# Later query maxima, key and value loads of layer 0 in pieces with two buffers, and a moved key copy in a two-layer attention backbone

## The chip, the cores and the metric

The kernel runs on one core of one Trainium2 chip. The metric is device time in microseconds (us) of one execution. The program is one launch of some 22,000 instructions on five engines: TensorE (PE: matrix products and transposes), VectorE (DVE), ScalarE (ACT), GpSimd (POOL) and SyncE (SP), which only issues DMA transfers. Each engine takes its instructions strictly in order; between engines they are tied by semaphores.

## The reference, cut to what matters

A context of 256 tokens and 1024 latent tokens (a 16 x 64 grid) of width 1024 pass through two layers. Each layer norms and modulates its input, projects it, runs two mixers side by side, gates them with SiLU and projects back.

```python
# layer 0 (even), for each of its two head groups A and B: 8 query heads, 2 key/value heads, head width 64
aq, ak, av, ag, bq, bk, bv, bg = split_cols(h @ w_in, EVEN_WIDTHS)
aq, ak = rms_norm(heads(aq), q_gain), rms_norm(heads(ak), k_gain)    # A alone; A and B get rotary
oa = gqa_attend(q_block, concat(c_ak, ak), concat(c_av, av))         # A: 128 queries against all 1280 keys
ob = gqa_attend(q_block, concat(c_bk, band of 384), ..., bias, sink) # B: context + window of +-128, a sink logit
y  = concat(oa * silu(ag), ob * silu(bg)) @ w_out
# layer 1 (odd): conformer convolution (C) and 2-D neighbourhood attention (D, 8 heads, 8 x 16 window + context)
y  = concat(conformer_conv(...), od * silu(dg)) @ w_out

def gqa_attend(q, k, v, bias, sink):
    s = einsum(q, k) * 64 ** -0.5 + bias
    return softmax(concat(s, sink)) @ v
```

Layer 0 also does the context rows; layer 1 updates the latent rows alone, and a last RMSNorm gives the output. All is float32.

## The kernel before, in words

Values keep float32 accuracy by being split into a high and a low part (`split`): a product is three matrix products of such parts. Everything that TensorE does is therefore in pieces of 128 x 128 by up to 512 columns.

**Layer 0** runs four *passes*, one for each pair of a mixer (B, then A) and a key/value head, in the sequence `ORDER = (2, 3, 0, 1)`. Ahead of a pass stands its projection, `fill0`: `proj_qkv` makes queries, keys and values for ten blocks of 128 tokens, and `proj_gate` the gate (the rest of it follows inside the pass). For each block `qk_tail` (L805 to L813) transposes queries and keys, splits them on ScalarE (`qs`), and SyncE writes them to DRAM: `Qd` at L812, `Kd` at L813. Values go to `Vd`, gates to `Gs`. The projections of the next pass are the *fill* that is woven into the attention of the pass that runs (`weave`): `NFILL = (39, 39, 36)` says how many steps of it.

A pass then has ten *groups*, one for each block of 128 queries (four heads wide, so 512 columns), in the sequence `QORD = (2, 3, 4, 0, 5, 6, 1, 7, 8, 9)`. A group is prepared by `attn_prep` (L365): it loads its queries (`load_q`: `QH`, twice the high part, and `QL`, the low part; three buffers each), makes its row maxima (`maxes`, products called `mx`, at L552 and below in layer 0 and at L1304 and below in layer 1, reduced on VectorE into `mp`), transposes the negated maxima (`trn`, L389) and writes them into `QL`. Then for each *key tile* of 128 keys `attn_gen` (L396) makes scores `st` from two products (L448 with the keys `KA`: high part in 64 partitions, low part in 64; L452 with `KB`: high part again, plus rows of ones that bring in the maxima), their exponential `pf` on ScalarE (L458 to L460), its two parts `ph` (ScalarE) and `pl` (VectorE or GpSimd), and, three tiles later (`flush`), three products with the values `V` into `ov` (L411 to L413). The last of a group's tiles ends with its normalisation and `finish`, which writes `Od`.

Groups are prepared two ahead: while group *g* runs through its key tiles, the preparation of *g*+2 advances with it, a few steps per tile (`g.step`); its first step issues the query load and the next four do nothing (`for _ in range(4): yield`).

The keys of a pass are loaded whole, when the pass's first group is prepared (`load_ka`, L520, two transfers of 64 x 1280 into one of two `KA` buffers) and when it starts (`load_kb`, L525, one more into the only `KB`); the values, whole, at its first `flush` (`load_v`, into the only `V` buffer).

**Layer 1** has sixteen groups (8 heads, two halves of 512 queries), with the projections of later heads and the output projection as fill. `load_head` (L1253) fetches the next head's keys at the start of a head's first group, and `load_k` (L359) does so with two transfers into `KA` and a copy of the high part into `KB` on ScalarE (L363).

What the program lists is not yet the order on the engines. The framework's scheduler builds each engine's order from the program's, by priorities and a timeline model of its own; the orders shown below are what it built.

Of the kernel before, what the change touches and what calls it, by code (L numbers as in the profile page):

```python
# [10 lines left out]
F32 = mybir.dt.float32  # L11
# [21 lines left out]
BMO = (0, 320, 320, 760)  # L33
LOOK0, LOOK1 = 3, 3
AHEAD = 3
BMB = 2
# [31 lines left out]
GB = 2  # L68
NFILL = (39, 39, 36)
GL = 12  # L70
# [18 lines left out]
def tile_kernel(ctx: ExitStack, tc: tile.TileContext, a, out):  # L89
# [268 lines left out]

    def load_k(k, kh, kl):  # L359
        KA, KB = Ks[k % len(Ks)]  # L360
        SY.dma_start(KA[0:64, :].bitcast(F32), kh)
        SY.dma_start(KA[64:128, :].bitcast(F32), kl)
        SC.copy(KB[0:64, :], KA[0:64, :].bitcast(F32))  # L363

    def attn_prep(pool, g):  # L365
# [28 lines left out]
    def attn_gen(pool, groups, vshare, look, nexts=None):  # L394
# [31 lines left out]

        for p in preps[:2]:
            for n_, _ in enumerate(p):
                if n_ % 2:
                    yield  # L430
        for gi, g in enumerate(groups):
            ids = [gi + 2] if gi + 2 < len(groups) else []
            if nexts is not None and gi in nexts:
                ids = nexts[gi]
            g.next = chain.from_iterable(preps[k] for k in ids)
            g.step = -(-18 * len(ids) // len(g.tiles))
        for g, t in items[:AHEAD]:
            g.ahead(t)
        for x, (g, t) in enumerate(items):
            if x + AHEAD < len(items):  # L440
                items[x + AHEAD][0].ahead(items[x + AHEAD][1])
            if t == 0:
                g.start()
            k, q0, n, extra = g.tiles[t]
            KA, KB = g.k()
# [30 lines left out]
            yield  # L476
# [40 lines left out]

    KAs, KBs = [None] * 4, [None] * 4

    def load_ka(u):  # L520
        KAs[u] = a0.tile([P, NTOK], F32R, tag="KA", name=nm("KAt"), bufs=2)
        SY.dma_start(KAs[u][0:64, :].bitcast(F32), Kd[u][:, 0, :])
        SY.dma_start(KAs[u][64:128, :].bitcast(F32), Kd[u][:, 1, :])

    def load_kb(u):  # L525
        KB = KBs[0]
        SY.dma_start(KB[0:64, :].bitcast(F32), Kd[u][:, 0, :])

    def group0(u, qb):
        isb = u >= 2  # L530

        first = qb == QORD[0]

        def load_q(QH, QL):
            if first:
                load_ka(u)
            src = Qd[u][qb].rearrange("(e d) s a t -> d s e (a t)", e=2)
            for dst, s in ((QH[0:64, :], 0), (QH[64:128, :], 0), (QL[0:64, :], 1)):
                SY.dma_start(dst.bitcast(F32).rearrange("d (e c) -> d e c", e=2), src[:, s])
# [6 lines left out]
        def maxes(QH, mp):  # L546
# [12 lines left out]
            for hd in range(4):  # L559
# [7 lines left out]
                else:  # L567
# [30 lines left out]
        def finish(ov, rb):  # L598
# [9 lines left out]
            else:  # L608
# [3 lines left out]

        hs = (u - 2) * 4
        g = Group(load_q=load_q, start=(lambda: load_kb(u)) if first else (lambda: None), bias=False, ahead=lambda t: None, gate=gate, v=lambda k: Vs[0][:, k, :], load_v=(lambda: SY.dma_start(Vs[0][:, :, 0:128].bitcast(F32), Vd[u])) if first else None, maxes=maxes, nmp=1 if qb < 2 else (2 if isb else 3),
                  sink=(sink[:, hs : hs + 4], sink8[:, hs : hs + 4]) if isb else None, skm=lambda: sk, k=lambda: (KAs[u], KBs[0]),
                  tiles=[(k, 0, 512, x) for k, x in kt], den=den, finish=finish)
# [6 lines left out]
    with ExitStack() as p0x:  # L623
# [181 lines left out]
        def qk_tail(u, j, pc):  # L805

            tr = bank("tr", nm("trk"))
            for i in range(3):
                PE.transpose(tr[:, i * P : (i + 1) * P], pc[:, i * P : (i + 1) * P], ident)
            qs = ap.tile([P, 2, 384], F32R, tag="qs", name=nm("qs"), bufs=2)  # L810
            split(tr[:, 0:384], qs[:, 0, :], qs[:, 1, :], "s", "v")
            SY.dma_start(Qd[u][j].rearrange("p a b t -> p a (b t)"), qs[:, :, 0:256].bitcast(F32))  # L812
            mark[0] = SY.dma_start(Kd[u][:, :, j * P : (j + 1) * P], qs[0:64, :, 256:384].bitcast(F32))  # L813

# [17 lines left out]
        def fill0(k, w=None):  # L832
            yield from proj_qkv(ORDER[k], w)
            yield from proj_gate(ORDER[k], gblocks(k)[0])

# [3 lines left out]
        while hold[0]:  # L839
            next(mods)  # L840
        v_tiles(a0, 10)
        KBs[0] = a0.tile([P, NTOK], F32R, tag="KB", name="KBt")
        GP.memset(KBs[0][64:68, :].bitcast(F32), 1.0)
        main = attn_gen(a0, [group0(u, qb) for u in ORDER for qb in QORD], VS0, LOOK0)
# [219 lines left out]
    with ExitStack():  # L1064
# [186 lines left out]
        od = [None, None]  # L1251

        def load_head(hd):  # L1253
            i, e = divmod(hd, 2)
            ds = slice(e * 64, (e + 1) * 64)
            load_k(hd, KD[i][ds, 0, :], KD[i][ds, 1, :])

        def group1(gi, hd, hf):
# [66 lines left out]
            def finish(ov, rb):  # L1325
# [6 lines left out]
                if i == 3:  # L1332
# [3 lines left out]

            g = Group(load_q=load_q, maxes=maxes, nmp=2, bias=True, ahead=ahead, sink=None, tiles=tiles, den=den, finish=finish,
                      start=start, gate=gate,
                      k=lambda: Ks[hd % len(Ks)], load_v=None, v=lambda k: Vs[gi % 2][:, k if k < 2 else k - 5 * hf, :])
# [4 lines left out]
        groups1 = [group1(gi, *x) for gi, x in enumerate(SEQ)]  # L1344
        load_head(0)
        x2, ocs, od3, fin = [], [], [], [0]

# [247 lines left out]
```

## Time and profile before

| | before |
|---|---|
| runs (us) | 1596.81, 1595.64, 1587.97; median 1595.64 |
| profiled execution (us) | 1590.95 |
| its span on the core (us) | 1589.2 |
| mean granted TensorE clock | 0.965 |
| bytes moved by DMA | 222 MB, mean 140 GB/s |

The profile is of one execution of its own, 1590.95 us of device time; the span is the part of it from the first to the last instruction. "Busy" is the time in which an engine executes, and what it waits for is told by the semaphore that ended the wait. In a row of the waits stand the engine, the operation and line that waited, what it waited for, then the total in us, the number of times and the longest. In a row of the timeline stand the start, the duration, the engine, the line, the operation, output <- inputs, shapes, and in brackets the idle time ahead of it with what ended that. The names are those of the program without their numbers: `KAt`, `KBt`, `Vt` are the tiles of keys and values, `Q`, `K`, `V`, `G` the DRAM buffers of layer 0, `QD`, `KD` those of layer 1.

### The profile page before, as it was taken

The numbers are of one execution on the slowest core, as the hardware profiler recorded it, in microseconds if no ns is written. First come the engines' busy times: TensorE is split into PE (matmuls) and PEld (weight loads), VectorE is DVE, ScalarE is ACT, GpSimd is POOL, SyncE is SP. The second block draws the span as 40 slices with busy tenths as digits, with TensorE's granted clock in tenths as the row PEclk, the third lists the DMA queues.
The fourth block names the chain that finished last, engine by engine and source line by source line (L and its number), as shares of the span: only waits on it lengthen the run. The fifth ranks groups of instructions, "written<-read, shape, count | busy, mean of one in ns | idle before, by whom it ended". The sixth has DMA issues, their size and how long they took to land.

```text
span 1589.2 us, 22236 instructions
## 1 busy us (share of the span) xinstructions
PE 1459.0 (92%) x6984; PEld 1180.6 (74%) x6984; DVE 1124.1 (71%) x2172; ACT 756.6 (48%) x1542; POOL 831.3 (52%) x760
## 2 busy tenths in 40 slices
PE   6789989998999988989999889999999999789895
PEld 1779867787778667767887768888887787577685
DVE  4898787588857668455478776999846467576676
ACT  2722353444434664654555564443433455545473
POOL 1561364455636667756654655754532334444575
PEclk9999999998999999989999989999999999799997
DMA  9548234532442123471111122213456878888732
GB/s 316 179 144 270 83 101 138 176 95 80 146 143 75 36 65 113 156 223 51 57 40 44 57 66 79 92 55 107 162 176 219 246 222 262 239 219 232 221 97 106
DMA packets 198462, 222.01 MB, mean 140 GB/s; under 512 B 18812, under 2 KB 154696, under 8 KB 198344
## 3 DMA queue, kind: packets, MB, share of 16 engines
q1 hardware_dynamic: 191680, 209.02, 42.9%
q10 hardware_dynamic: 6664, 11.57, 2.4%
q8 instruction: 55, 0.90, 0.2%
q14 instruction: 63, 0.52, 0.1%
HBM read 160.49 MB, written 60.03 MB: 139 GB/s over the span
## 4 chain that ended last, share of the span: by engine, by line
PE 61%; DVE 15%; DMA 13%; issue 4%; POOL 3%; SPq 2%; ACT 1%; DVEq 0%; POOLq 0%; ACTq 0%
PE p L320 6%; PE p L319 6%; PE p L321 6%; PE ov L411 4%; PE ov L413 4%; PE ov L412 3%; PE po L320 3%; PE po L319 3%; PE po L321 3%; PE st L448 3%; PE st L452 3%; DMA mw<-in_mod_w_dram 3%; DMA QH<-QD 2%; PE pq L321 2%; PE pq L319 2%
## 5 line engine op out<-in xcount | busy, mean ns | idle before, releaser
L300 POOL TENSOR_TENSOR pl<-pf,ph 128x512 fp32r<-128x512 f32 (+4 forms) x321 | 394.1, 1239 | 304.4 <-ACT ph L297 252.4
L300 POOL TENSOR_TENSOR wl<-wr,wh 128x256 fp32r<-128x256 f32 (+2 forms) x256 | 199.3, 794 | 218.2 <-ACT wh L297 209.4
L460 ACT ACTIVATE pf<-st 128x512 f32<-128x512 f32 x284 | 166.2, 596 | 171.3 <-PE st L452 126.5
L297 ACT CAST ph<-pf 128x512 fp32r<-128x512 f32 (+4 forms) x364 | 209.9, 588 | 38.4 <-PE ov L412 22.0
L297 ACT CAST wh<-wr 128x256 fp32r<-128x256 f32 (+2 forms) x264 | 103.4, 404 | 162.4 <-DMA wr<-in_od_d_dram 38.6
L319 PE MATMUL p<-hh,wh 128*128 128x512 f32 x448 | 177.2, 397 | 2.4 <-DVE spk L300 1.4
L320 PE MATMUL p<-hl,wh 128*128 128x512 f32 x448 | 178.4, 399 | 0.4 <-POOL hl L300 0.4
L321 PE MATMUL p<-hh,wl 128*128 128x512 f32 x448 | 173.3, 396 | 0.2 <-POOL wl L300 0.2
L411 PE MATMUL ov<-ph,Vt 128*128 128x512 f32 (+4 forms) x364 | 144.8, 398 | 15.4 <-DVE y L602 8.2
L413 PE MATMUL ov<-pl,Vt 128*128 128x512 f32 (+4 forms) x364 | 144.5, 397 | 7.5 <-POOL pl L300 5.5
L448 PE MATMUL st<-QH,KAt 128*128 128x512 f32 (+4 forms) x364 | 142.5, 393 | 5.4 <-ACT pf L460 3.4
L412 PE MATMUL ov<-ph,Vt 128*64 128x512 f32 (+4 forms) x364 | 142.0, 390 | 0.0
L452 PE MATMUL st<-QL,KBt 68*128 68x512 f32 (+4 forms) x364 | 137.5, 387 | 0.7 <-DVE QL L390 0.7
L1081 DVE SCALAR_TENSOR_TENSOR cps<-U,taps,cps 128x512 f32<-128x512 f32 x184 | 124.3, 747 | 0.0
L565 DVE TENSOR_REDUCE mp<-mx 128x1 f32<-128x512 f32 x128 | 85.9, 683 | 49.7 <-PE mx L564 49.1
L220 DVE SCALAR_TENSOR_TENSOR macc<-mw,csil,macc 128x512 f32<-128x512 f32 x107 | 93.1, 889 | 23.5 <-DMA mw<-in_mod_w_dram 21.4
L319 PEld LDWEIGHTS p<-hh,wh 128*128 128x128 f32 x448 | 84.1, 188 | 23.4 <-DVE spk L300 1.6
L321 PEld LDWEIGHTS p<-hh,wl 128*128 128x128 f32 x448 | 84.4, 189 | 20.5 <-POOL wl L300 0.6
L320 PEld LDWEIGHTS p<-hl,wh 128*128 128x128 f32 x448 | 84.2, 188 | 19.5 <-POOL hl L300 0.8
L411 PEld LDWEIGHTS ov<-ph,Vt 128*128 128x128 f32 x364 | 71.9, 197 | 32.9 <-issue 8.6
L413 PEld LDWEIGHTS ov<-pl,Vt 128*128 128x128 f32 x364 | 71.6, 197 | 31.5 <-POOL pl L300 8.5
L321 PE MATMUL pq<-wh,hl 128*128 128x384 f32 x256 | 88.7, 348 | 1.1 <-DVE hl L311 0.7
(276 smaller groups left out, 3521.5 us busy)
## 6 DMA issues: line engine op xcount, KB each, us to landing
mw<-in_mod_w_dram SPq DMA_DIRECT2D x34, 512.0 KB, 5.6
Q<-qs SPq DMA_DIRECT2D x40, 256.0 KB, 2.7
QH<-Q SPq DMA_DIRECT2D x80, 128.0 KB, 2.8
wr<-in_od_d_dram SPq DMA_DIRECT2D x64, 128.0 KB, 2.9
mw<-in_mod_w_dram SPq DMA_DIRECT2D x28, 256.0 KB, 3.3
wr<-in_ev_qkv_dram SPq DMA_DIRECT2D x32, 192.0 KB, 3.4
KAt<-KD SPq DMA_DIRECT2D x16, 384.0 KB, 6.1
wr<-in_od_wo_dram SPq DMA_DIRECT2D x48, 128.0 KB, 3.0
```

What stands on the lines that cost most here:

```text
L297: SC.copy(hi, src)
L300: (GP if leng == "g" else VE).tensor_tensor(lo, src, hi.bitcast(F32), op=ALU.subtract)
L319: PE.matmul(o, lh, rh, start=first, stop=False)
L320: PE.matmul(o, lh, rl, start=False, stop=False)
L321: done[0] = PE.matmul(o, ll, rh, start=False, stop=last)
L411: PE.matmul(o, V[:, 64:192], ph[:, :n], start=(t == 0), stop=False)
L412: PE.matmul(g.ov[0:64, q0 : q0 + n], V[:, 0:64], ph[:, :n], start=False, stop=False)
L413: pvs.append(PE.matmul(o, V[:, 64:192], pl[:, :n], start=False, stop=(last and g.sink is None)))
L448: sts.append(PE.matmul(st[:, :n], KA[:, cs], g.QH[:, q0 : q0 + n], start=True, stop=False))
L452: PE.matmul(st[:, :n], KB[0:68, cs], g.QL[0:68, q0 : q0 + n], start=False, stop=True)
L460: SC.activation(pf[:, :n], st[:, :n], AF.Exp, scale=1.0 if g.bias else SCALE)
L1081: VE.scalar_tensor_tensor(pc, uc, w, pc, op0=ALU.mult, op1=ALU.add)
```

## The change

- **Preparation** (`attn_prep`, `attn_gen`): at the first key tile of a group all the query loads that belong to it are issued at once. The rest of a preparation is put in a queue and begins `LEAD` key tiles later, three in layer 0 and four in layer 1, with `g.rate` steps per tile (2 in A, 3 in B and in layer 1). What is left over is finished before the group that needs it starts.
- **Keys and values of layer 0**: `K` in DRAM has 128 partitions (high part, low part), so that one transfer fills `KA`. `KB` and `V` have two buffers. Both are fetched in three pieces (blocks 0 and 1; 2 to 5; 6 to 9), each when `qk_tail` has written the block behind its end (`PIECES`). `KB` is a copy of `KA` on ScalarE, asked for at the last tile of the last group but one of the pass before (`last`); the first pass loads it from DRAM.
- **Fill**: `fill0` finishes the transposes of a projection before its gate product; `NFILL` is 43, 43, 40.
- **Layer 1**: the copy into `KB` is asked for at the last tile of a head's first half, no longer right behind the load.
- The ring of tiles for the modulation weights at the start borrows `KB` and `V` with two buffers each.

```diff
+LEAD = (3, 4)
...
-NFILL = (39, 39, 36)
+NFILL = (43, 43, 40)
...
-                        bufs=2 if t == "A" else 1)
+                        bufs=2)
...
-    def load_k(k, kh, kl):
+    def load_k(k, ks):
         KA, KB = Ks[k % len(Ks)]
-        SY.dma_start(KA[0:64, :].bitcast(F32), kh)
-        SY.dma_start(KA[64:128, :].bitcast(F32), kl)
-        SC.copy(KB[0:64, :], KA[0:64, :].bitcast(F32))
+        for s_ in range(2):
+            SY.dma_start(KA[s_ * 64 : (s_ + 1) * 64, :].bitcast(F32), ks[:, s_])
+        return KA, KB
...
         g.load_q(QH, QL)
-        for _ in range(4):
-            yield
+        yield
...
+        work = []
+        def prepare(x, n):
+            while n and work and work[0][0] <= x:
+                if next(work[0][1], work) is work:
+                    work.pop(0)
+                else:
+                    n -= 1
...
             if t == 0:
                 g.start()
+                while any(p is g.prep for _, p in work):
+                    prepare(len(items), 1)
+                for k in g.ids:
+                    next(preps[k])
+                    work.append((x + LEAD[layer[0]], preps[k]))
+            rate = g.rate * max(len(work), 1)
...
-            for _ in range(g.step // 2):
-                next(g.next, None)
+            if t == len(g.tiles) - 1:
+                g.last()
+            prepare(x, rate // 2)
             yield
             if len(pend) > look:
                 flush()
-            for _ in range(g.step - g.step // 2):
-                next(g.next, None)
-            if t == len(g.tiles) - 1:
-                for _ in g.next:
-                    pass
+            prepare(x, rate - rate // 2)
             yield
...
-    Kd = [dram(f"K{u}", [64, 2, NTOK]) for u in range(4)]
+    Kd = [dram(f"K{u}", [P, NTOK]) for u in range(4)]
...
-    def load_ka(u):
+    PIECES = {1: (0, 2), 5: (2, 6), 9: (6, 10)}
+    both = []
+    def kv_tiles(u):
+        if not both:
+            for _ in range(2):
+                both.append((a0.tile([P, NTOK], F32R, tag="KB", name=nm("KBt"), bufs=2),
+                             a0.tile([P, 10, 192], F32R, tag="V", name=nm("Vt"), bufs=2)))
+                GP.memset(both[-1][0][64:68, :].bitcast(F32), 1.0)
+                GP.memset(both[-1][1][:, :, 128:192].bitcast(F32), 1.0)
         KAs[u] = a0.tile([P, NTOK], F32R, tag="KA", name=nm("KAt"), bufs=2)
-        SY.dma_start(KAs[u][0:64, :].bitcast(F32), Kd[u][:, 0, :])
-        SY.dma_start(KAs[u][64:128, :].bitcast(F32), Kd[u][:, 1, :])
-    def load_kb(u):
-        KB = KBs[0]
-        SY.dma_start(KB[0:64, :].bitcast(F32), Kd[u][:, 0, :])
+        KBs[u], V0s[u] = both[ORDER.index(u) % 2]
+    def load_kv(u, j0, j1):
+        ts = slice(j0 * P, j1 * P)
+        SY.dma_start(KAs[u][:, ts].bitcast(F32), Kd[u][:, ts])
+        SY.dma_start(V0s[u][:, j0:j1, 0:128].bitcast(F32), Vd[u][:, j0:j1])
+    def copy_k(KA, KB):
+        SC.copy(KB[0:64, :], KA[0:64, :].bitcast(F32))
...
+        def last():
+            if qb == QORD[-2] and u != ORDER[-1]:
+                v = ORDER[ORDER.index(u) + 1]
+                copy_k(KAs[v], KBs[v])
...
-            mark[0] = SY.dma_start(Kd[u][:, :, j * P : (j + 1) * P], qs[0:64, :, 256:384].bitcast(F32))
+            mark[0] = SY.dma_start(Kd[u].rearrange("(s d) t -> d s t", s=2)[:, :, j * P : (j + 1) * P],
+                                   qs[0:64, :, 256:384].bitcast(F32))
+            if j == 0 and not solo[0]:
+                kv_tiles(u)
+            if j in PIECES and not solo[0]:
+                load_kv(u, *PIECES[j])
...
             yield from proj_qkv(ORDER[k], w)
+            while tails and k:
+                qk_tail(*tails.pop(0))
+                yield
             yield from proj_gate(ORDER[k], gblocks(k)[0])
...
+            def last():
+                if hf == 0 and hd < 7:
+                    copy_k(*heads[hd + 1])
```

**What moves on the engines.** On SyncE, around the last head change of layer 0 (`K1_140` is the DRAM buffer of the fourth pass's keys, `KAt_1710` their tile, `Q1_2` and `Q1_3` the queries of its first two groups), the order before is:

```order
L539 DMA QH_1708_6812<-Q1_2_111 64x2x256 x2
L539 DMA QL_1709_6813<-Q1_2_111 64x2x256
L812 DMA Q1_6_115<-qs_1643_6589 256x1x256
L813 DMA K1_140<-qs_1643_6589 128x1x128
...
L812 DMA Q1_9_118<-qs_1683_6739 256x1x256
L813 DMA K1_140<-qs_1683_6739 128x1x128
L522 DMA KAt_1710_6814<-K1_140 64x1280
L523 DMA KAt_1710_6814<-K1_140 64x1280
L330 DMA wr_1904_7514<-in_ev_wo_dram 128x256
L330 DMA wr_1907_7520<-in_ev_wo_dram 128x256
L539 DMA QH_1770_6993<-Q1_3_112 64x2x256 x2
L539 DMA QL_1771_6994<-Q1_3_112 64x2x256
```

And of the changed kernel, at the same place (`KAt_1384` is the tile now, and the load its last piece, 512 keys):

```order
L843 DMA Q1_9_118<-qs_1584_6432 256x1x256
L844 DMA K1_140<-qs_1584_6432 64x2x128
L638 DMA Od_154<-y_1635_6576 128x2x128
L569 DMA gt_1681_6740<-G0_147 128x2x128
L553 DMA KAt_1384_5695<-K1_140 128x512
...
L331 DMA wr_1912_7539<-in_ev_wo_dram 128x256
L331 DMA wr_1915_7545<-in_ev_wo_dram 128x256
L565 DMA QH_1707_6820<-Q1_2_111 64x2x256 x2
L565 DMA QL_1708_6821<-Q1_2_111 64x2x256
```

Before, the keys stand behind the last key block's write and behind the queries of the pass's first group; now their last piece stands behind that write and ahead of those queries.

On ScalarE of the changed kernel, the copy into `KBt` for the fourth pass (L557, from `KAt_1384`) stands among the exponentials (`pf`) and their high parts (`ph`), four instructions behind the cast that makes the last block of queries and keys (`qs_1584`, the one that SyncE writes above):

```order
L298 CAST ph_1622_6532<-pf_1624_6534 128x512
L298 CAST hh_1890_7480<-hl_1891_7481 128x1024
L298 CAST qs_1584_6432<-trk_1583_6428 128x384
L298 CAST hh_1890_7480<-hl_1891_7481 128x1024 x2
L341 ACTIVATE sg_1867_7356<-pg_1858_7305 128x512
L557 CAST KBt_207_1258<-KAt_1384_5695 64x1280
L479 ACTIVATE pf_1631_6562<-st_1628_6557 128x512
L479 ACTIVATE pf_1639_6595<-st_1636_6590 128x512
L341 ACTIVATE sg_1876_7405<-pg_1868_7360 128x512
```

Before there is no such instruction in layer 0. On TensorE in layer 1, at the maxima of the third group (`mx1`, from the queries `QH_3346`), the order before is:

```order
L448 MATMUL st_3352_13501<-QH_3228_13026,KAt_3025_12363 128x256
L452 MATMUL st_3352_13501<-QL_3229_13027,KBt_3026_12364 128x256
L389 MATMUL trn_3325_13391<-ident_68,nmt_3320_13367 4x128
...
L1191 MATMUL trv_3565_14249<-ident_68,vT_3523_14080 128x128 x4
L413 MATMUL ov_3319_13363<-pl_3339_13452,Vt_3030_12370 128x512
L1304 MATMUL mx1_3358_13517<-KAt_3027_12366,QH_3346_13476 128x256 x2
L1312 MATMUL mx1_3359_13521<-KAt_3027_12366,QH_3346_13476 128x440
```

And of the changed kernel (`QH_3344` are the same group's queries):

```order
L389 MATMUL trn_3353_13499<-ident_68,nmt_3342_13468 4x128
L467 MATMUL st_3355_13516<-QH_3226_13029,KAt_3028_12379 128x256
L471 MATMUL st_3355_13516<-QL_3227_13030,KBt_3029_12380 128x256
...
L1232 MATMUL trv_3567_14262<-ident_68,vT_3526_14095 128x128 x4
L413 MATMUL ov_3315_13358<-pl_3340_13463,Vt_3033_12386 128x512
L1351 MATMUL mx1_3407_13656<-KAt_3030_12382,QH_3344_13479 128x256 x2
L1359 MATMUL mx1_3408_13672<-KAt_3030_12382,QH_3344_13479 128x440
```

These maxima stand at the same place of the built order in both.

More of the change, by code (lines that the diff above doesn't have):

```diff
@@ L427, in attn_gen @@
         for p in preps[:2]:
+            next(p)
+            yield
+        for _ in range(2):
+            yield
+        for p in preps[:2]:
             for n_, _ in enumerate(p):
@@ L430, in attn_gen @@
                     yield
+        work = []
[5 more added lines that the diff above has]
+                    n -= 1
         for gi, g in enumerate(groups):
-            ids = [gi + 2] if gi + 2 < len(groups) else []
+            g.ids = [gi + 2] if gi + 2 < len(groups) else []
             if nexts is not None and gi in nexts:
-                ids = nexts[gi]
-            g.next = chain.from_iterable(preps[k] for k in ids)
-            g.step = -(-18 * len(ids) // len(g.tiles))
+                g.ids = nexts[gi]
         for g, t in items[:AHEAD]:
@@ L840, in tile_kernel @@
             next(mods)
[L841 to L843 removed]
+        assert not tails
+        kv_tiles(ORDER[0])
+        for j in PIECES:
+            load_kv(ORDER[0], *PIECES[j])
+        SY.dma_start(KBs[ORDER[0]][0:64, :].bitcast(F32), Kd[ORDER[0]][0:64])
         main = attn_gen(a0, [group0(u, qb) for u in ORDER for qb in QORD], VS0, LOOK0)
@@ L1335, in finish @@
                 SY.dma_start(O1d[ds, i, hf], y[ds])
-            g = Group(load_q=load_q, maxes=maxes, nmp=2, bias=True, ahead=ahead, sink=None, tiles=tiles, den=den, finish=finish,
-                      start=start, gate=gate,
+            g = Group(load_q=load_q, maxes=maxes, nmp=2, bias=True, rate=3, ahead=ahead, sink=None, tiles=tiles, den=den, finish=finish,
+                      start=start, gate=gate, last=last,
                       k=lambda: Ks[hd % len(Ks)], load_v=None, v=lambda k: Vs[gi % 2][:, k if k < 2 else k - 5 * hf, :])
```

15 lines of the change are left out of this document (8 added, 7 removed).

## The prediction

> **What bounds the kernel.** I read the page's busy shares first, then the chain that ended last, then TensorE's waits, then the stretches of time around the longest of them.
>
> ```profile
> span 1589.2 us, 22236 instructions
> PE 1459.0 (92%) x6984; PEld 1180.6 (74%) x6984; DVE 1124.1 (71%) x2172; ACT 756.6 (48%) x1542; POOL 831.3 (52%) x760
> PE 61%; DVE 15%; DMA 13%; issue 4%; POOL 3%; SPq 2%; ACT 1%; DVEq 0%; POOLq 0%; ACTq 0%
> ```
>
> TensorE is busy 92% of the span and carries 61% of the chain; a transfer carries 13%. The change alters no product, so all that it can win is time in which TensorE stands, or runs slowly. The list of waits says for what (us, times, longest):
>
> ```profile
> PE mx L1304 <- DMA QH<-QD: 12.4, 7, 2.9
> PE mx L552 <- DMA KAt<-K: 9.1, 2, 5.8
> PE mx L552 <- DMA QH<-Q: 7.0, 5, 2.4
> PE mx L1304 <- issue: 2.7, 1, 2.7
> PE ov L411 <- DMA Vt<-V: 0.8, 1, 0.8
> ```
>
> The change speaks to all of these: queries of layer 1 (QH<-QD), and keys, queries and values of layer 0. Together they are 32.0 us. Which of them fall at a head change of layer 0 is seen in TensorE's timeline; the bracket is the idle time ahead and what ended it.
>
> ```profile
> 166.15 1.09 PE L552 MATMUL mx<-KAt,QH 128*128 128x256 f32 x4 [3.29 <-DMA KAt<-K]
> ...
> 311.61 0.71 PE L552 MATMUL mx<-KAt,QH 128*128 128x256 f32 x4 [2.36 <-DMA QH<-Q]
> ...
> 470.15 0.55 PE L552 MATMUL mx<-KAt,QH 128*128 128x256 f32 x1 [2.08 <-DMA QH<-Q]
> ...
> 684.47 1.19 PE L552 MATMUL mx<-KAt,QH 128*128 128x256 f32 x4 [5.79 <-DMA KAt<-K]
> ```
>
> These are the first maxima of the four head passes (3.29, 2.36, 2.08, 5.79 us). SyncE's timeline shows why the third and the fourth come late: keys are loaded only after the last key block was written, and in the third the second half of QH is queued behind them.
>
> ```profile
> 460.33 0.63 SPq L813 DMA_DIRECT2D K<-qs  x1
> 461.05 0.54 SPq L330 DMA_DIRECT2D wr<-in_ev_qkv_dram  x1
> 461.69 0.62 SPq L539 DMA_DIRECT2D QH<-Q  x1
> 463.49 0.48 SPq L522 DMA_DIRECT2D KAt<-K  x1
> 464.03 0.59 SPq L523 DMA_DIRECT2D KAt<-K  x1
> 464.67 0.60 SPq L539 DMA_DIRECT2D QH<-Q  x1
> ...
> 672.15 1.23 SPq L813 DMA_DIRECT2D K<-qs  x1
> ...
> 675.35 0.49 SPq L522 DMA_DIRECT2D KAt<-K  x1
> 675.89 0.59 SPq L523 DMA_DIRECT2D KAt<-K  x1
> ```
>
> **Key and value loads of layer 0 (in pieces, double buffered).** In the order of the changed kernel the last piece of the fourth pass's keys stands eleven rows ahead of its queries; before, the keys came fourteen rows behind them. It waits for the same last K write, but that write now comes earlier against the attention, because the transposes of a projection are finished before its gate product. By PE rows (one matmul each) the pass's first maxima stand 2877 rows into the program against 2883. For the second and third passes the keys no longer stand between K write and QH on SyncE. I take these three waits as gone: 5.79 + 2.36 + 2.08 = 10.2 us, and the 0.8 us for values with them, since the values are loaded in pieces while the pass before still runs: 11.0. What covers them is the attention of the pass before; if a piece is late it costs what it costs now, so the bounds are 0 and -11.0.
>
> The first pass cannot load earlier than its own last K write. Its first maxima stand 14 matmuls earlier in TensorE's order, so TensorE arrives there sooner and waits longer by 14 products; the values no longer go ahead of the keys. Bounds: gone (-3.3), or longer by 14 products at 0.23 us (+3.2, pitch below). I take 0.
>
> **The clock.** After such a wait TensorE's products follow each other at half the pace, and the granted clock of the stretch falls.
>
> ```profile
> 308.16 0.39 PE L452 MATMUL st<-QL,KBt 68*128 68x512 f32 x1
> 308.39 0.39 PE L413 MATMUL ov<-pl,Vt 128*128 128x512 f32 x1
> ...
> 686.74 0.63 PE L448 MATMUL st<-QH,KAt 128*128 128x512 f32 x1
> 687.17 0.63 PE L452 MATMUL st<-QL,KBt 68*128 68x512 f32 x1
> ...
> 312.00:332.00 20.00, 20.00 (x99) 18.08 (x98) 16.41 (x38) 8.79 (x19) 8.76 (x7) 0.91 0.32 96
> 470.00:490.00 20.00, 19.84 (x96) 18.06 (x97) 13.49 (x21) 8.85 (x19) 10.99 (x9) 0.91 0.16 47
> 524.00:544.00 20.00, 19.13 (x75) 13.32 (x74) 11.75 (x23) 13.32 (x23) 12.89 (x11) 0.91 0.12 34
> 680.00:700.00 20.00, 15.27 (x61) 11.56 (x62) 9.77 (x19) 9.82 (x18) 10.81 (x10) 0.83 0.98 284
> 724.00:744.00 20.00, 20.00 (x96) 16.10 (x95) 10.22 (x17) 8.91 (x19) 12.75 (x12) 1.00 0.15 47
> 744.00:764.00 20.00, 20.00 (x102) 16.31 (x101) 9.24 (x17) 10.93 (x22) 13.17 (x12) 1.00 0.17 53
> ```
>
> The starts lie 0.23 us apart at full clock (308.16, 308.39) and 0.43 in the slow stretch (686.74, 687.17). The columns of the stretches are its length, the five engines (PE first, with its number of instructions), clock, share of DMA, GB/s. A clock of 0.91 over 20 us is 1.8 us lost, in the two stretches that follow the waits of 2.36 and 2.08 us; in the one with 0.83 it is 3.4 us, of which about half fell on the wait itself. 1.8 + 1.8 + 1.7 = 5.3 us, if the waits go; bounds 0 and -5.3. I take all of it, for both short waits show it.
>
> The Trainium skill, "TensorE: Matmul & The Clock Gate", section "What's actually happening", puts the half-rate state after at least one idle window of about 3.4 us. This trace differs: the clock also fell after gaps of 2.36 and 2.08 us. By the page only the gap of 5.79 us would have lowered it, and the sum below would be 3.6 us higher.
>
> **Key copy on ScalarE.** Three loads of 320 KB into KB are replaced by a copy KA to KB on ScalarE. Layer 1 has done the same since before:
>
> ```profile
> L363 ACT CAST KBt<-KAt x8: 1471/1472/1480, 1239.1 to 1476.1; 64x1536 fp32r<-64x1536 f32 x8
> ...
> ACT KBt L363 <- DMA KAt<-KD: 19.8, 7, 5.3
> ...
> PE ov L411 <- ACT ph L297: 2.7, 1, 2.7
> ```
>
> By columns a copy of 1280 takes 1472 x 1280/1536 = 1227 ns (an estimate). The program asks for it at the last tile of the last group but one, but the built order puts it about 2 us of TensorE's work behind the last piece's load, just as in layer 1, where ScalarE, which works in order, waited 19.8/7 = 2.8 us each. So ScalarE is held 2.8 + 1.2 = 4.0 us three times. Behind it wait the next exponentials, and TensorE for those. At the first two copies gate and projection products cover it. At the third, some ten matmuls stand behind it that need no new exponential, 10 x 0.23 = 2.3 us, so 1.7 us show. Bounds: 0, and all with the longest wait, 3 x (5.3 + 1.2) = 19.5. I take 1.7, nearest to the mean row.
>
> In layer 1 the copy's hook moves too, but its built place does not: it still stands directly behind the load, one or two tiles later in two heads. 0.
>
> **The lead of the maxima.** In the program the maxima of the next but one group now begin three or four key tiles after its load. In the built order they do not: in layer 1 the number of score tiles between the start of a group and the first maxima was 2, 3, 1, 3, 2, 2, 2, 3 and is 2, 3, 1, 1, 2, 2, 5, 0 for the first eight groups prepared there. Only priorities changed; the maxima are still taken where the scheduler believes the queries have landed. A load cannot start earlier either: its buffer is free only when the group three before has made its last scores. So the 12.4 + 2.7 us of layer 1 stay, as do the 2.5 us (7.0 - 2.36 - 2.08, smaller ones) in layer 0. Bounds: all gone (-15.1 and about 3 of clock), or a tile more of lateness in two groups (+3). I take 0.
>
> **Fill.** Since transposes come ahead of the gate product, projections run 60 to 70 matmuls further ahead of the attention from the second pass on. Near row 2400 some 50 rows of attention without fill disappear; in the last hundred rows before the final normalisation (3840 to 3940) there were 32 output products, and now there are none. The stretch without fill at 524 holds 75 instructions in 20 us, of which the clock of 0.91 took 1.8: 18.2/75 = 0.243 us each. Those with fill hold 96 and 102: 0.202 each. (100 - 50) x 0.041 = +2.0 us. Bounds: 0, and 100 at the crowded stretch's 61 in 20 us (0.328), +12.6.
>
> The remaining edits cost nothing on the path: K is written in the same 64 KB, two more transfers per pass (six for four) lie beside products, two more memsets on GpSimd stand ahead of the first attention, where it is half idle, and the modulation weights gain a buffer at two of the six places of their ring, while their loads, which go out in order, are still held by the other four.
>
> **Sum.** The profiled execution took 1590.95 us: - 11.0 - 5.3 + 1.7 + 2.0 = - 12.6, so 1578.4. The median shown, 1595.64, lies 4.7 us above it (runs from 1587.97 to 1596.81), so an equal shift leaves the changed median between 1578.4 and 1583.0; I say 1581.
>
> **Rivals.**
> 1. *Slower: the key copies take the loads' place.* If each copy holds ScalarE the longest wait and TensorE has no cover, and loses clock after it, each costs 5.3 + 1.2 + 1.8 = 8.3 us, 24.9 in place of 1.7: 1604. For it speaks that the third copy stands only four instructions behind the cast that makes the last keys; against it, that layer 1 has eight such copies, and the most that ScalarE's exponentials ended of TensorE's waits from 1235 us on is the one of 2.7 us above. From 4.8 us each (12.6 + 1.7 over 3) the gain is gone.
> 2. *No difference: the gain is given back at the end of layer 0,* where attention runs alone. At the crowded rate, +12.6 in place of 2.0, 1592. It is for this that no product is left to fill in; against it, that the crowded stretch also held a wait of 5.79 us.
> 3. *The lead works as written,* in layer 1 too: 15.1 us and some 3 of clock less, 1563. The built order speaks against it.
> 4. *The clock does not come back with the two short waits,* if something else in those stretches lowered it: 3.6 us less is won, 1585. Against it: the clock is 1.00 in the two stretches without such a gap. The page named above would have it this way.
>
> **Chances.** Forecast 0.50; rival 1 0.12; rival 2 0.20; rival 3 0.10; rival 4 0.08. About 0.5% (8 us) is what a measurement can tell here. Against 1595.64 the forecast's own spread of some 6 us is mostly below 1587.7: 0.44 of its 0.50, all of rival 3, 0.07 of rival 4 and 0.03 of rival 2 make 0.64 faster; rival 1 is 0.10 slower; the rest, 0.26, the same. The range reaches from near rival 3 to beyond rival 2: 1566 to 1598.
>
> **What would show it.** Right: the first maxima of passes two to four start without a bracket of more than 0.5 us, the clock there is 1.00, KB copies on ScalarE wait 2 to 4 us, and the layer 1 line "QH<-QD" stays near 12 us. Wrong: gaps of TensorE ended by ScalarE near the copies, fewer than 60 instructions per 20 us at the end of layer 0, or QH<-QD of layer 1 below 5 us.

## The result, and the profile after

The changed kernel takes 1571.14 us (median of six runs, 1563.54 to 1572.46) against 1596.22 us for the kernel before: a ratio of 0.9833, 95% interval 0.9811 to 0.9856. It is faster by 25 us by the medians and by 27 by the ratio; the forecast was 1581 us, 15 us less than the median shown. The profiled execution took 1571.46 us, so it stands at its median, while that of before lay 5 us below its own.

The page of the changed kernel: span, busy time of the engines, and the chain that ended last by engine.

```profile
span 1569.6 us, 22251 instructions
PE 1460.8 (93%) x6984; PEld 1178.9 (75%) x6984; DVE 1129.4 (72%) x2172; ACT 762.0 (49%) x1545; POOL 830.0 (53%) x762
PE 65%; DVE 14%; DMA 11%; issue 4%; POOL 2%; SPq 2%; ACT 1%; ACTq 0%; DVEq 0%; POOLq 0%
```

The span is 19.6 us shorter, at the same number of matmuls. Layer 1 begins with the first product `p<-hh,wh` of its projection, at 951.83 us before and 929.45 us after, so layer 0 alone is 22.4 us shorter, and the rest is 2.8 us longer (637.4 and 640.2 us). Stretches of time show what layer 0 won. First the kernel before: from 60 us to the end of layer 0, and its last 431 matmuls (columns: stretch, its length, the five engines with PE first, granted clock, share of DMA, GB/s).

```profile
60.00:951.80 891.80, 828.68 (x4035) 680.65 (x4034) 640.65 (x1202) 432.83 (x874) 493.80 (x407) 0.97 0.35 106
846.80:951.80 105.00, 94.85 (x431) 73.64 (x429) 81.94 (x135) 59.18 (x120) 61.51 (x58) 0.93 0.17 56
```

The same of the changed kernel:

```profile
60.00:929.40 869.40, 820.08 (x4037) 673.88 (x4036) 645.65 (x1202) 440.65 (x877) 494.91 (x410) 0.97 0.35 106
818.50:929.40 110.90, 100.13 (x431) 75.28 (x430) 85.58 (x143) 69.67 (x135) 70.11 (x65) 0.92 0.17 54
```

In layer 0 TensorE stands 49.3 us where it stood 63.1 (length less busy time), and is busy 820.1 us where it was busy 828.7, with the same products: 13.8 us less waiting and 8.6 us less of busy time. Of the latter the granted clock explains 6.8: its mean, rounded to 0.97 in both rows, is 0.966 before and 0.973 after, so that the slow clock took 30.7 and 23.9 us of the stretch. Behind matmul 3750 or so, where only attention is left, 431 matmuls take 5.9 us longer; so up to there the change won 28 us. By numbers of matmuls (counted from 0 in the order of their starts), 5.2 of the 28 lie ahead of matmul 700, by when the first pass's maxima have begun; 4.0, 3.7 and 3.8 around the three other head changes (1300 to 1500, 2000 to 2200, 2900 to 3100); and the other 12 between them, for which no single reason is shown.

TensorE's waits in layer 0 of the changed kernel for transfers of queries, keys and values:

```profile
PE mx L578 <- DMA QH<-Q: 2.9, 3, 1.5
PE mx L578 <- DMA V<-vs: 0.4, 1, 0.4
```

They answer to 9.1 + 7.0 + 0.8 us before: 16.9 has become 3.3. All other waits of layer 0 together stayed at 45 us. The first maxima of the four passes, in TensorE's timeline (the bracket, where there is one, is the idle time ahead and what ended it):

```profile
160.06 0.35 PE L578 MATMUL mx<-KAt,QH 128*128 128x256 f32 x1 [0.42 <-DMA V<-vs]
...
308.70 0.28 PE L578 MATMUL mx<-KAt,QH 128*128 128x256 f32 x1
...
457.33 0.28 PE L578 MATMUL mx<-KAt,QH 128*128 128x256 f32 x1
...
659.64 0.39 PE L578 MATMUL mx<-KAt,QH 128*128 128x256 f32 x2
```

Before, they waited 3.29, 2.36, 2.08 and 5.79 us. At the fourth, SyncE's and ScalarE's timelines show the distance: the last K write is issued at 616.46, the last piece of the keys at 621.11, the copy runs at 624.74, and the queries are loaded at 649.59, ten microseconds ahead of their use.

```profile
616.46 0.62 SPq L844 DMA_DIRECT2D K<-qs  x1
...
621.11 0.60 SPq L553 DMA_DIRECT2D KAt<-K  x1
...
624.74 1.26 ACT L557 CAST KBt<-KAt 64x1280 fp32r<-64x1280 f32 x1 [4.53 <-DMA KAt<-K]
...
649.59 1.54 SPq L565 DMA_DIRECT2D QH<-Q  x2
```

Before, the last K write was issued at 672.15, 12 us ahead of the maxima; now it is 43 us ahead.

### The profile page after: what moved, and what is told of

Same layout as the page of the kernel before. It is cut to its first block, busy times and chain, and to the rows that moved or that the text cites. A ratio compares the mean times of both kernels' runs of the same rounds, so it can differ in the third digit from the quotient of the medians.

```text
span 1569.6 us, 22251 instructions
## 1 busy us (share of the span) xinstructions
PE 1460.8 (93%) x6984; PEld 1178.9 (75%) x6984; DVE 1129.4 (72%) x2172; ACT 762.0 (49%) x1545; POOL 830.0 (53%) x762
## 4 chain that ended last, share of the span: by engine, by line
PE 65%; DVE 14%; DMA 11%; issue 4%; POOL 2%; SPq 2%; ACT 1%; ACTq 0%; DVEq 0%; POOLq 0%
PE p L322 6%; PE p L321 6%; PE p L320 6%; PE ov L411 4%; PE ov L413 4%; PE ov L412 4%; PE po L320 4%; PE po L321 4%; PE po L322 4%; PE st L467 4%; PE st L471 4%; DMA mw<-in_mod_w_dram 3%; DVE macc L221 2%; PE pq L322 2%; PE pq L321 2%
## 5 line engine op out<-in xcount | busy, mean ns | idle before, releaser
L320 PEld LDWEIGHTS p<-hh,wh 128*128 128x128 f32 x448 | 84.6, 189 | 23.6 <-DVE spk L301 1.7
L322 PEld LDWEIGHTS p<-hh,wl 128*128 128x128 f32 x448 | 84.8, 189 | 20.1 <-POOL wl L301 0.6
L467 PEld LDWEIGHTS st<-QH,KAt 128*128 128x128 f32 x364 | 71.2, 196 | 33.4 <-ACT pf L479 17.6
```

Source lines behind the costliest of these rows:

```text
L320: PE.matmul(o, lh, rh, start=first, stop=False)
L322: done[0] = PE.matmul(o, ll, rh, start=False, stop=last)
L467: sts.append(PE.matmul(st[:, :n], KA[:, cs], g.QH[:, q0 : q0 + n], start=True, stop=False))
```

## The experiments

The change has three parts that can be built apart: the *loads* of layer 0 (pieces, two buffers, `KB` copied on ScalarE), the *lead* (preparation), and the *fill* (transposes ahead of the gate product, and `NFILL`). The fourth, layer 1's copy, is no part: with the copy put back right behind the load, the built order of all five engines is the same, row for row.

| kernel | loads | lead | fill | median us | ratio to before (95%) | layer 0 ends in its trace, us |
|---|---|---|---|---|---|---|
| before | | | | 1594.85 to 1596.22 | | 951.8 |
| loads_alone | x | | | 1594.88 | 0.9988 (0.9964 to 1.0012) | 949.0 |
| lead_alone | | x | | 1579.28 | 0.9908 (0.9880 to 0.9936) | 940.7 |
| fill_alone | | | x | 1587.18 | 0.9945 (0.9922 to 0.9969) | 951.0 |
| nfill_alone | | | pace only | 1587.01 | 0.9945 (0.9923 to 0.9967) | 949.0 |
| lead_and_fill | | x | x | 1578.28 | 0.9892 (0.9863 to 0.9922) | 934.5 |
| no_fill | x | x | | 1583.35 | 0.9938 (0.9915 to 0.9961) | 942.9 |
| no_fill_kb_dma | x, no copy | x | | 1576.00 | 0.9869 (0.9844 to 0.9893) | 934.6 |
| no_lead | x | | x | 1575.45 | 0.9861 (0.9835 to 0.9888) | 930.8 |
| lead_layer1 | x | layer 1 only | x | 1569.19 | 0.9831 (0.9805 to 0.9857) | 931.2 |
| late_tails | x | x | pace only | 1575.16 | 0.9867 (0.9835 to 0.9898) | 932.8 |
| kb_dma | x, no copy | x | x | 1570.30 | 0.9860 (0.9823 to 0.9896) | 935.2 |
| nfill_47 | x | x | more | 1567.32 | 0.9830 (0.9800 to 0.9860) | 931.6 |
| the change | x | x | x | 1571.14 | 0.9833 (0.9811 to 0.9856) | 929.4 |

The profiled executions of fill_alone and nfill_alone were 5 to 6 us above their medians, so their last column may be too high by up to that; a difference of a few us between two single traces proves little. Gains in us below are ratios times 1596, unless they are called medians'; what stands behind +- is half of a 95% interval. Layer 1 and the end took 629.9 to 642.9 us in these traces. Each edit of layer 0 also lets the scheduler build another order for layer 1, so single traces are compared in layer 0.

**One part each, and the copy.** The first runs asked what the loads do alone, what the lead does alone, what is left without the fill, and what the copies of `KB` cost.

```diff
 loads_alone (on the changed kernel: preparation, fill and layer 1 as before)
+        for _ in range(4):
+            yield
...
-NFILL = (43, 43, 40)
+NFILL = (39, 39, 36)
```

> Only the key and value part of the change in layer 0 is done (two buffers, pieces, KB by ScalarE copy, K with 128 partitions); preparation, fill and layer 1 are those of before. Theory A (the head changes: loads of keys and values that no longer come last) expects nearly the whole gain: layer 0 as in the changed kernel, and the 6 us that its end lost given back, 1565 to 1571 us, with the first maxima of passes 2 to 4 without a gap of TensorE over 0.5 us. Theory B (the lead of the maxima made a good part of the gain) expects 1581 us or more, 10 us over the changed kernel. Theory C (transposes ahead of the gate product bring the keys in time) expects the fourth pass's gap of 5.8 us and its slow clock to be back, 1580 us or more.

Theory A, which is the prediction's, falls: no gain that can be told from none. TensorE's waits in layer 0 of this trace say why. Those for transfers fell by 10.1 us, to 6.8, and the others grew by 8.7. Around the fourth head change:

```profile
671.50 0.51 PE L414 MATMUL ov<-pl,Vt 128*128 128x512 f32 x1 [2.37 <-POOL pl L301]
...
675.99 1.26 ACT L554 CAST KBt<-KAt 64x1280 fp32r<-64x1280 f32 x1 [2.67 <-DMA KAt<-K]
...
676.10 1.19 PE L587 MATMUL mx<-KAt,QH 128*128 128x512 f32 x2 [1.96 <-DMA KAt<-K]
...
689.85 0.50 PE L459 MATMUL st<-QH,KAt 128*128 128x512 f32 x1 [2.41 <-ACT pf L471]
```

The first maxima (at 666.62, without a wait) need only the first piece; the next ones need the last piece, which comes no earlier than before, because the last K write does not. ScalarE's copy waits for the same piece.

```diff
 lead_alone (on the kernel before: attn_prep and attn_gen of the change)
+LEAD = (3, 4)
...
```

> Only the preparation is changed (query loads at once, the rest three or four key tiles later); loads of keys and values, fill and layer 1's copy are those of before. Theory A expects no difference from before, 1591 to 1601 us, with the four gaps at the first maxima of layer 0's passes still there (13.5 us together) and the waits of layer 1 for QH near 12 us. Theory B expects a gain of 10 us or more, 1586 us or less. Theory C expects no difference.

Theory B: 15 us. Nothing but the preparation differs from before. The waits at the first maxima of passes 1 to 3 are gone, that of the fourth stays:

```profile
318.20 0.40 PE L566 MATMUL mx<-KAt,QH 128*128 128x256 f32 x2
...
472.74 0.40 PE L566 MATMUL mx<-KAt,QH 128*128 128x256 f32 x2
...
672.61 0.55 PE L566 MATMUL mx<-KAt,QH 128*128 128x256 f32 x1 [4.73 <-DMA KAt<-K]
```

Counted in the traces, the first maxima are TensorE's matmul 1402 and 2120 here, and 1356 and 2089 before: 46 and 31 matmuls later. In the program the keys' load goes out at once, and TensorE comes for it that much later. This is not all of the gain, though: the three waits made 7.7 us, but the stretches around the second and third head changes (matmuls 1300 to 1500 and 2000 to 2200) are 2.2 and 1.4 us shorter, and 7.9 of the 11.1 us that layer 0 won lie between matmuls 2200 and 2900, at no head change. Why the lead pays there is not shown.

```diff
 no_fill (on the changed kernel)
-NFILL = (43, 43, 40)
+NFILL = (39, 39, 36)
...
-            while tails and k:
-                qk_tail(*tails.pop(0))
-                yield
```

> The changed kernel with the fill of before: transposes stand behind the gate product again, and NFILL is 39, 39, 36. Theory A expects the 6 us at the end of layer 0 given back and the rest kept: 1563 to 1568 us, the stretch of the last 300 matmuls of layer 0 as fast as before. Theory C expects the head changes' gaps back, 1580 us or more.

Theory C: 17 us of the 27 are gone (12 of 25 between the medians). In the trace the copy of the fourth pass's keys runs later than the pass's first maxima (662.51), and holds the exponentials that TensorE needs:

```profile
668.37 1.26 ACT L557 CAST KBt<-KAt 64x1280 fp32r<-64x1280 f32 x1 [4.28 <-DMA KAt<-K]
669.53 0.59 ACT L479 ACTIVATE pf<-st 128x512 f32<-128x512 f32 x1
...
670.17 0.80 PE L467 MATMUL st<-QH,KAt 128*128 128x512 f32 x1 [3.47 <-ACT pf L479]
```

But this wait is not what the 17 us are: from matmul 2900 to 3100, around it, this kernel takes 52.7 us and the changed one 52.8. The 13.5 us by which its layer 0 is longer lie earlier, 5.4 of them around the second head change (1300 to 1500), 4.2 from 700 to 1300 and 4.0 from 2200 to 2900.

```diff
 kb_dma (on the changed kernel)
-                copy_k(KAs[v], KBs[v])
...
+            SY.dma_start(KBs[u][0:64, ts].bitcast(F32), Kd[u][0:64, ts])
```

> The changed kernel with KB of passes 2 to 4 loaded from DRAM in the same three pieces, in place of the copy on ScalarE. If the copies cost what the prediction put down, 1.7 us, 1568 to 1572 us. If each holds ScalarE and TensorE behind it for its whole wait and duration (10.4 us of waiting and 3 x 1.26 us in the changed kernel's trace), 1557 to 1561 us. If the nine more transfers of 64 partitions delay the queries, 1574 us or more.

No difference that can be told (0.0027 +- 0.0043, in favour of the copies): in the changed kernel they cost nothing that shows, though they hold ScalarE for 10.4 us of waiting and 3.8 us of copying.

**Which parts need each other.** Theory D puts the parts together, theory E says that the fill makes the lead needless.

```diff
 no_lead: the changed kernel with attn_prep's four yields and g.step of before
 lead_layer1: the changed kernel with
-LEAD = (3, 4)
+LEAD = (0, 4)
```

> The changed kernel with the preparation of before (no LEAD, steps spread evenly over the group); loads, fill and the moved copy of layer 1 kept. Theory D (three parts that need each other: the lead puts the first maxima of passes 2 and 3 some 30 to 50 matmuls later in TensorE's order, the early loads serve passes 1 and 4, and the transposes ahead of the gate product put the copies of the keys under projection products) expects the waits of passes 2 and 3 back in part, 1577 to 1584 us. Theory E (with the transposes ahead the keys and queries are there in any case, and the lead adds nothing) expects 1569 to 1573 us.

> The changed kernel with LEAD = (0, 4): no lead in layer 0, the full one in layer 1. Theory D expects most of the lead's gain to lie in layer 0, so 1576 to 1584 us, the gain lost by the end of layer 0 and layer 1 as in the changed kernel. If the lead pays in layer 1, 1569 to 1573 us. Theory E expects 1569 to 1573 us too.

The first lies between the two theories, the second where E has it. Against the changed kernel the lead is worth 0.0028 of the time, with a half-interval of 0.0035 (from the two ratios' own): not shown. With LEAD 0 in layer 0 nothing is lost (the queue of preparations and its rate stay there). That it pays in layer 1 instead isn't seen there either: TensorE waits 10.6 us for QH<-QD in lead_layer1, 9.6 in no_lead and 9.0 in the changed kernel. So D falls where it made the lead one of three parts that need each other. Beside one part alone the lead does pay: 8 us with the loads (0.9938 against 0.9988) and 8 with the fill (0.9892, below, against 0.9945), each +- 6.

```diff
 no_fill_kb_dma: the edits of no_fill and of kb_dma
 lead_and_fill: the kernel before with the lead and the fill
```

> The changed kernel with the fill of before and with KB loaded from DRAM in place of the copies on ScalarE. If what the changed kernel loses without the new fill (12 us) is ScalarE held by the copies at the head changes, the loss is gone: 1568 to 1574 us. If it is the late keys and queries themselves, it stays: 1580 to 1587 us.

> The kernel before with the lead and the new fill, keys and values loaded as before (whole, KB and V with one buffer, KB by a third load). Theory D expects the early loads to be worth the fourth pass's wait and its slow clock, 6 to 8 us: 1576 to 1580 us. If the transposes ahead alone bring the keys in time, 1569 to 1573 us, and the new loads are worth nothing.

Without the fill, keys for `KB` from DRAM in place of the copies win 11 us (0.9869 against 0.9938), +- 5.4. TensorE's waits for ScalarE's exponentials, of no_fill and then of no_fill_kb_dma:

```profile
PE st L467 <- ACT pf L479: 16.4, 16, 3.5
```

```profile
PE st L467 <- ACT pf L479: 9.1, 12, 1.8
```

So the edit pays. That it pays because the copies hold ScalarE is argued, not shown: the three copies of no_fill waited 1.20, 0.18 and 4.28 us, yet from matmul 2900 to 3100, around the third, no_fill takes 52.7 us and no_fill_kb_dma 54.9, while 5.7 of the 8.3 us by which the latter's layer 0 is shorter lie in its last 431 matmuls, behind all copies.

The second kernel's time fell between the two ranges: of the 17 us lost without the fill 11 go with the copies and 6 stay (0.0036 +- 0.0033). Against kb_dma, which has the fill and no copies either, it is 0.0009 +- 0.0044: without the copies the fill is not shown to pay. In lead_and_fill the loads of before cost 9 us, +- 6 (7 between the medians), about as D had it.

**What in the fill.** The fill has two edits: transposes ahead, and 10% more steps per key tile.

```diff
 fill_alone, nfill_alone: the kernel before with
-NFILL = (39, 39, 36)
+NFILL = (43, 43, 40)
...
 and fill_alone with this as well, which late_tails takes out of the changed kernel
+            while tails and k:
+                qk_tail(*tails.pop(0))
+                yield
 nfill_47: the changed kernel with
-NFILL = (43, 43, 40)
+NFILL = (47, 47, 44)
```

> The kernel before with the new fill alone: transposes ahead of the gate product and NFILL 43, 43, 40. Theory F (what counts is that a projection is through earlier against the attention, so that keys, queries and copies of the next pass have time; each other part gets rid of the same waits) expects most of the gain, 1576 to 1583 us. If the fill only pays through the new loads, as the loads only paid with it, 1590 to 1599 us.

> The kernel before with NFILL 43, 43, 40 alone, transposes where they were, so that ten per cent more steps of the projection are done per key tile. If the pace is what counts in the fill, as in the run with the whole of it, 1576 to 1583 us. If it is the place of the transposes, 1590 to 1599 us.

> The changed kernel without the transposes ahead of the gate product; NFILL stays 43, 43, 40. If the pace is what counts, 1569 to 1575 us, as the changed kernel. If it is the place of the transposes, 1579 to 1587 us, as with the whole fill undone.

> The changed kernel with NFILL 47, 47, 44: a projection is through earlier still. If waits at the head changes are still to be won, 1563 to 1568 us. If what is won there is lost where the fill has run out, as the prediction's term for the fill has it, 1572 to 1580 us.

Alone, the fill wins 9 us, less than theory F wanted and more than its rival allows, and the pace alone wins the same. In the changed kernel, with the transposes back behind the gate product, 4 us between the medians are lost (0.0034 +- 0.0039: not shown). So in the times the pace does all that can be told, and a share of the transposes is not shown. A faster pace still has its median in the range named for waits still to be won, but differs from the changed kernel by 0.0003 +- 0.0038: nothing that can be told.

In the traces the two edits do different things. This is the time from the issue of a pass's last K write to the pass's first maxima, in us:

| pass | before | nfill_alone | fill_alone | late_tails | the change |
|---|---|---|---|---|---|
| second | 10.0 | 16.6 | 33.3 | 23.2 | 34.0 |
| third | 9.8 | 23.7 | 19.2 | 24.4 | 23.6 |
| fourth | 12.3 | 13.7 | 39.0 | 20.1 | 43.2 |

With the pace but no transposes ahead (nfill_alone, and late_tails with loads and lead) most is won at the third pass; the transposes add at the second and, above all, at the fourth. In nfill_alone the fourth pass's last write still comes late. Its keys are asked for at 665.99, when that write has landed (665.92), and TensorE stands ahead of the first maxima; the bracket names no semaphore, but the second half of the keys landed at 674.93:

```profile
661.35 0.61 SPq L813 DMA_DIRECT2D K<-qs  x1
662.06 0.60 SPq L539 DMA_DIRECT2D QL<-Q  x1
665.99 0.48 SPq L522 DMA_DIRECT2D KAt<-K  x1
...
675.02 0.55 PE L552 MATMUL mx<-KAt,QH 128*128 128x256 f32 x1 [10.30 <-issue]
```

In fill_alone, with the same loads of before, the write stands 39 us ahead and the first maxima do not wait:

```profile
637.75 0.68 SPq L813 DMA_DIRECT2D K<-qs  x1
...
676.75 0.40 PE L552 MATMUL mx<-KAt,QH 128*128 128x256 f32 x2
```

From matmul 2900 to 3100 fill_alone takes 47.0 us, nfill_alone 58.5 and the kernel before 56.6. Why fill_alone is no faster than nfill_alone as a whole is open: it gives 10.8 us back between matmuls 1500 and 2000 and 6.9 in the last 431.

No variant is clearly faster than the changed kernel.

## Why the prediction was right, and where it was wrong

The time lies within the range, and the gain was 25 us by the medians where 15 were forecast. Term by term, in layer 0's traces:

- **Waits for transfers: right in kind, not in cause.** -11.0 forecast, -13.6 measured (16.9 to 3.3). The difference is the first pass, taken as 0: its 3.29 us went too. At the three other head changes waits and clock together were to give 15.5 us (10.2 and 5.3), and the stretches around them are 11.5 shorter. But the step "I take these three waits as gone" credited the loads, and the loads alone win 0.0012 +- 0.0024. "What covers them is the attention of the pass before" was the condition, and it does not hold without the fill: the last piece then comes as late as the whole did. Given the fill, the loads win 13 us (0.9861 against 0.9945) or 9 us (0.9833 against 0.9892 with the lead), each +- 6, close to the size forecast. One reading was off without harm: at the second and third passes the last piece of the keys still stands between the last K write and QH (433.77, 435.96 and 452.54 us at the third), but long ahead of the latter.
- **The clock: right, a little small.** -5.3 forecast; by the granted clock 6.8 us less were lost in layer 0. The stretches at the second and third head changes now have a clock of 1.00, and so does the one behind the fourth:

```profile
300.00:320.00 20.00, 20.00 (x105) 17.76 (x105) 17.75 (x29) 11.28 (x22) 15.48 (x11) 1.00 0.17 51
450.00:470.00 20.00, 20.00 (x103) 17.59 (x102) 11.83 (x22) 12.51 (x27) 15.42 (x13) 1.00 0.25 77
560.00:580.00 20.00, 17.12 (x79) 13.07 (x77) 12.97 (x25) 11.44 (x24) 13.66 (x14) 0.83 0.30 88
640.00:660.00 20.00, 16.14 (x60) 11.81 (x61) 4.91 (x11) 12.46 (x23) 16.09 (x16) 0.83 0.76 252
660.00:680.00 20.00, 20.00 (x97) 16.21 (x96) 10.61 (x19) 10.93 (x21) 13.01 (x12) 1.00 0.20 60
```

So rival 4 did not come true. But what was held against it, a clock of 1.00 where there is no such gap, leaves out the stretch 524 to 544 of the kernel before, which the prediction shows with 0.91: no gap of TensorE in it is longer than 0.35 us.

- **The key copy: right, with the fill.** ScalarE waited 3.5 us each in the mean (2.8 forecast), though 0.67, 5.25 and 4.53 singly, none of them within the 2 to 4 us named as a sign; with or without the copies the time is the same. Without the fill the three copies go with 11 us, so a price in the kind of rival 1's is not ruled out there; that it is ScalarE being held is not shown.
- **The lead: right in sum, wrong in reason.** 0 forecast, 0.0028 +- 0.0035 measured beside the other two parts. But "in the built order they do not" begin later was read in layer 1, and for layer 0 at the fourth pass alone (2877 against 2883); the second and third passes' maxima do stand later, by 54 and 16 matmuls (in no_lead by 75 and 4, so the fill and the loads move them too). Alone the lead wins 15 us, among it waits that the other parts remove as well. Layer 1's waits for queries fell from 12.4 to 9.0 us; most stayed, as forecast, so rival 3 did not come true.
- **The fill: the step that failed.** +2.0 forecast. The loss where the fill has run out is there, 5.9 us for the last 431 matmuls against the 4.1 us put down for a hundred bare rows, though in no_fill only 2.2 of it come back; rival 2 had put up to 12.6 there. What was missed is the other side: the fill is worth 9 us alone (0.9945) and 17 us in the change (0.9833 against 0.9938). The term counted where products lie beside the attention, and not that the next pass's keys, queries and copies get more time between the last K write and their first use, 43 us in place of 12 at the fourth pass. The prediction saw the earlier write, and put it down to the transposes; the traces bear that out at the second and fourth passes, while the third owes it to the pace. How much time each distance saves is not shown: fill_alone and nfill_alone take the same time with very different distances, and no_fill, with 2.4 us at the fourth pass, is as fast around it as the changed kernel.

That the sum came out within 10 us is in part luck: an overvalued loads term stood in for a fill term of the wrong sign, and some 12 of the 28 us won ahead of layer 0's end lie between the head changes, where no term looked for them. Loads and lead together (no_fill, 0.9938) are no faster than the lead alone (0.9908), and without the copies they are, barely beyond the noise (0.9869, a difference of 0.0039 +- 0.0037). Open is what parts no_lead from lead_layer1, whose intervals overlap.

## What to carry to other kernels

Early loads pay only as far as what they load is written early: before crediting them, find the last write in the queue's timeline and ask what moves *it* (here the fill: the pace of the projection that feeds it, and the place of its transposes). Several edits that remove one wait cannot be added up; build each alone and each left out before a gain is given to any. And compare the traces stretch by stretch, by number of matmul: a wait that vanishes at one place need not be where the time was won. Look up a moved position in the built order at every place that the sum rests on, not at one of four.

## What the hardware showed unexpectedly

The granted clock falls after shorter or broken waits than one would think. In the changed kernel the stretch from 640 us has a clock of 0.83, with 60 matmuls in 20 us, though its two longest gaps are 1.80 and 1.11 us:

```profile
564.94 0.80 PE L590 MATMUL mx<-KAt,QH 128*128 128x512 f32 x1 [2.83 <-DVE mp L591]
...
643.43 0.80 PE L467 MATMUL st<-QH,KAt 128*128 128x512 f32 x1 [1.80 <-ACT pf L479]
...
657.02 0.47 PE L411 MATMUL ov<-ph,Vt 128*128 128x512 f32 x1 [1.11 <-DVE y L633]
```

The stretch from 560 us, with the gap of 2.83 us, has 0.83 too. From 640 us on the clock falls to half within the first of the two gaps, and is back before the second:

```profile
636.00:642.60 6.60, 4.38 (x17) 2.68 (x17) 4.19 (x7) 2.13 (x5) 6.60 (x6) 1.00 0.92 290
642.60:649.40 6.80, 5.97 (x16) 4.70 (x17) 0.69 (x1) 3.49 (x7) 4.14 (x4) 0.50 0.97 331
```

The Trainium skill, "TensorE: Matmul & The Clock Gate", section "What's actually happening", speaks of at least one idle window of about 3.4 us; these rows differ from it, as those of the kernel before did. So 13.8 us less of waiting came with 6.8 us less of slow clock.

A load of keys has no fixed price either. The transfers of a stretch (number, KB each, median us from issue to landing; here of one landing each), around the third and the fourth head change of the kernel before:

```profile
KAt<-K SPq DMA_DIRECT2D x2, 320.0 KB, 3.9
...
KAt<-K SPq DMA_DIRECT2D x2, 320.0 KB, 6.9
```

And around the fourth in nfill_alone:

```profile
KAt<-K SPq DMA_DIRECT2D x2, 320.0 KB, 8.4
```
